# One scan for both directions of the S5 heads, and one modulation buffer lent by S5

## The chip, the cores and the metric

The kernel runs on one core of a Trainium2 chip. The metric is device time in microseconds (us) of one execution. TensorE (PE in the profile) multiplies matrices, VectorE (DVE) and ScalarE (ACT) work on tiles in on-chip memory, GpSimd (POOL) here clears memory and issues transfers, and SyncE (SP) issues transfers.

## What is computed

One layer of a hybrid backbone over 256 latent tokens and 256 context tokens of width 2048. Modulation vectors (shift, scale, gate) come from a matrix-vector product of SiLU(c) with a 2048 x 12288 matrix. A combined input projection feeds three mixers: S5 (a diagonal state space model), a convolution module, and a bidirectional mLSTM with four heads. An output projection, a SwiGLU block of width 5632 and a final norm follow.

The change is in S5 and in the buffers of the modulation. S5 has 32 groups of 16 channels with 64 complex states each, and it runs in both directions:

```
lam_bar = exp(lam * exp(log_step));  b_bar = ((lam_bar - 1) / lam)[..., None] * b
for di, reverse in enumerate((False, True)):
    h_c, h_fin = scan(einsum(uc, b_bar), lam_bar, 0, reverse)        # context
    h_x, _     = scan(einsum(ux, b_bar), lam_bar, h_fin, reverse)    # latent
    y_x += real(einsum(h_x, c_mat))
```

## The kernel before

**Weights.** A stream of 386 chunks of 8 weight tiles (512 KB each) is read by SP into `raw` (3 buffers). ScalarE rounds a chunk into `whi` (`split`, L263), VectorE makes the rest `wlo` = raw - whi, and TensorE multiplies with both. The buffers of `whi` and `wlo` are 3 deep, so ScalarE and VectorE run at most three chunks ahead of TensorE. The stream goes through the stages in a fixed order (`tile_order`): input projection for S5 and part of k, conv, rest of k, v, q, o, then the S5 gate, the output projection and the SwiGLU blocks.

**Order.** Work beside the stream is written as generators (`conv_job`, `s5_job`, `mod_job`, `gates_job`, `attention`). At each chunk `Sched.pump` runs steps of them by priority, as long as its own running sums of VectorE's and ScalarE's estimated work are less than 3,500 ns ahead of TensorE's. The helpers (`tt`, `stt`, `scan`, `act`) add the estimates. Afterwards the framework orders each engine's instructions once more by a simulated time, so the order on an engine is fixed when the program is built. Within an engine the instructions run in that order.

**S5.** `s5_params` makes the constants. `s5_moves` spreads the projection over `U` with eight copies on ScalarE and eight on VectorE. `s5_job` then goes through 16 pairs; a pair has two units `u`, one for each direction. `prep(p)` makes the input matrices (`bb`, then products with the powers `LW` into `Wb`), the output matrices (`cc`, products with `LC` into `Mb`) and a table of sines and cosines (`tab`). `main5(p)` multiplies on TensorE, rotates the result by the table on VectorE (`Vr`), runs the decay recurrence with `scan` (L191; four scans of 128 elements, one for each direction and for real and imaginary part), rotates back (`H1`, `H2`), and multiplies with `Mb` on TensorE. `prep(p + 1)` and `main5(p)` are stepped in turn. At the end of the job 16 copies on ScalarE and 16 on VectorE gather the result into `gT`.

**Modulation.** The first third of the matrix is read during the input projection in 64 pieces of 512 KB, into seven buffers: four of the tag `wm` and three slices of tiles that have no other use yet (`wm_extra`). The rest is read in 128 pieces during the later stages, through the four `wm` buffers alone, by POOL's queue (L337). `mod_job` goes through it in four quarters. Quarter 0 is multiplied on TensorE. In the quarters 1 to 3 ScalarE starts an accumulator `macc` and VectorE adds piece after piece to it (L179, two instructions to a piece); every eight pieces four transposes on TensorE close a block (L755). Each step takes two pieces and then issues the next two transfers. A transfer waits on POOL until its buffer has been read.

Of the kernel before, what the change touches and what calls it, by code (L numbers as in the profile page):

```python
# [10 lines left out]
F32 = mybir.dt.float32  # L11
# [139 lines left out]
def hybrid_layer_kernel(ctx: ExitStack, tc: tile.TileContext, xt, ctxt, wm1, wmr, wst, wg, bvrow, pvd, cstd, s5p, out):  # L151
# [169 lines left out]


    wm = {}
    NWM = 4

    wm_extra = [pre.tile([128, 2048], F32, name="wmu", tag="U"), pre.tile([128, 2048], F32, name="wmt", tag="T1")]
    wm_t1 = wm_extra[1]
    wm_extra = [wm_extra[0][:, 0:1024], wm_extra[0][:, 1024:2048], wm_extra[1][:, 1024:2048]]
    NWX = NWM + len(wm_extra)

    def wm_dma(key, src, q=None):
# [109 lines left out]

    LW = pre.tile([128, 2, 32, 4], F32, name="LW")
    LC = pre.tile([128, 2, 32, 5], F32, name="LC")
    s5c = pre.tile([128, 4, 32], F32, name="s5c")
    fre, fim, rho, frac = (s5c[:, i, :] for i in range(4))

    def s5_params():
        a = wm_t1[:, 0:1024].rearrange("p (a b) -> p a b", a=32)
# [70 lines left out]
        for o, s1, x1, x2, op in ((fre, 0, ar, ai, OP.add), (fim, 0, ai, ar, OP.subtract)):  # L519
            tt(o, x1, lre, OP.mult)  # L520
            tt(q, x2, lim, OP.mult)
            tt(o, o, q, op)
            tt(o, o, iv, OP.mult)
        yield

        L = [None] * 5
# [243 lines left out]
        while mst["q"] <= q:  # L770
            sc.step(mj)

    for _ in range(4):
        mod_dma()
    mj = sc.add(mod_job(), P_MOD)

# [10 lines left out]
                    acopy(o, i)  # L787

    def s5_job():
        Wb = pre.tile([128, 2, 2, 4, 32], F32, name="Wb", tag="s5W")  # L790
        Mbs = [pre.tile([128, 2, 2, 5, 32], F32, name="Mb", tag="s5M", bufs=2) for _ in range(2)]
        G.memset(Wb, 0.0)
        for m in Mbs:
            G.memset(m, 0.0)
        P5 = {}
# [1 line left out]
        def prep(p):  # L797
            u0 = 2 * p
            Mb = Mbs[p % 2]
            bc = pre.tile([128, 2, 4, 16], F32, name="bc", tag="s5bc")  # L800
            nc.gpsimd.dma_start(bc, s5p[p])
            yield S5_Y[0]
            bb = pre.tile([128, 2, 2, 2, 16], F32, name="bb", tag="s5bb")
            cc = pre.tile([128, 2, 2, 2, 16], F32, name="cc", tag="s5cc")

            def fb(f):
                return f[:, u0:u0 + 2][:, :, None, None].to_broadcast([128, 2, 2, 16])
            t1 = tmp(64).rearrange("p (u r c) -> p u r c", u=2, r=2)
            t2 = tmp(64).rearrange("p (u r c) -> p u r c", u=2, r=2)
            tt(t1, fb(fre), bc[:, :, 0:2, :], OP.mult)  # L810
            tt(t2, fb(fim), bc[:, :, 0:2, :], OP.mult)
            tt(bb[:, 0, :, 0, :], t1[:, :, 0, :], t2[:, :, 1, :], OP.subtract)
            tt(bb[:, 0, :, 1, :], t1[:, :, 1, :], t2[:, :, 0, :], OP.add)
            act(bb[:, 1, :, 0, :], bb[:, 0, :, 1, :], AF.Copy, scale=-1.0)
            acopy(bb[:, 1, :, 1, :], bb[:, 0, :, 0, :])
            acopy(cc[:, 0, :, 0, :], bc[:, :, 2, :])
            act(cc[:, 0, :, 1, :], bc[:, :, 3, :], AF.Copy, scale=-1.0)
            act(cc[:, 1], bc[:, :, 3:1:-1, :], AF.Copy, scale=-1.0)
            yield
            for L, n, x, dst in ((LW, 4, bb, Wb), (LC, 5, cc, Mb)):  # L820
                d1, d2 = (tmp(64 * n).rearrange("p (u s c) -> p u s c", u=4, s=n) for _ in range(2))
                for o, i in ((d1, 0), (d2, 1)):
                    for u in range(2):
                        tt(o[:, 2 * u:2 * u + 2], L[:, i, u0 + u, :][:, None, :, None].to_broadcast([128, 2, n, 16]),
                           x[:, i, u][:, :, None, :].to_broadcast([128, 2, n, 16]), OP.mult)
                tt(d1, d1, d2, OP.add)
                for hh in range(2):
                    acopy(dst[64 * hh:64 * hh + 64, :, :, :, 16 * hh:16 * hh + 16].rearrange("p u r s c -> p (u r s) c"),
                          d1[64 * hh:64 * hh + 64].rearrange("p u s c -> p (u s) c"))
                yield  # L830
            tab = pre.tile([128, 2, 2, 128], F32, name="tab", tag="s5tab")
# [25 lines left out]
            acopy(M2, ps[:, 0:128])  # L857
            P5[p] = (Mb, Wi, M2, tab)
            yield S5_Y[2]

        def main5(p):
            u0 = 2 * p
            Mb, Wi, M2, tab = P5.pop(p)
            ps = bbank()
            pv4 = ps.rearrange("p (u r k) -> p u r k", u=2, r=2)
            for d in range(2):
                r = U[:, p, :]
                if d:
                    r = r.rearrange("p (h k) -> p h k", h=2)[:, :, ::-1]
                for ri in range(2):  # L870
                    mm(pv4[:, d, ri, :], Wi[:, d, ri, :], r, True, True, native=True)
            Vr = pre.tile([128, 2, 2, 128], F32, name="Vr", tag="s5V")
            P2 = tmp().rearrange("p (u r k) -> p u r k", u=2, r=2)
            tt(Vr, pv4, tab[:, :, 0:1, :].to_broadcast([128, 2, 2, 128]), OP.mult)
            tt(P2, pv4[:, :, ::-1, :], tab[:, :, 1:2, :].to_broadcast([128, 2, 2, 128]), OP.mult)
# [8 lines left out]
            H1 = tmp(256).rearrange("p (u r k) -> p u r k", u=2, r=2)  # L884
            H2 = tmp(256).rearrange("p (u r k) -> p u r k", u=2, r=2)
            tt(H1, Vr[:, :, :, 63:127], tab[:, :, 0:1, 63:127].to_broadcast([128, 2, 2, 64]), OP.mult)
            tt(H2, Vr[:, :, ::-1, 63:127], tab[:, :, 1:2, 63:127].to_broadcast([128, 2, 2, 64]), OP.mult)
            tt(H1[:, :, 0, :], H1[:, :, 0, :], H2[:, :, 0, :], OP.subtract)
            tt(H1[:, :, 1, :], H1[:, :, 1, :], H2[:, :, 1, :], OP.add)
            yield S5_Y[3]  # L890
            ps = bbank()
            for d in range(2):
                for ri in range(2):
                    h = H1[:, d, ri, :]
# [531 lines left out]
```

## Time and profile before

| | |
|---|---|
| median of 3 runs | 1460.43 us (1458.61 to 1460.6) |
| profiled execution, its own time | 1461.92 us |
| span of its trace | 1460.2 us |
| TensorE busy | 1416.0 us (97%) |
| VectorE busy | 1058.8 us (73%) |
| ScalarE busy | 740.4 us (51%) |
| mean granted TensorE clock | 0.99 |

The span runs from the first to the last instruction; the profiled execution's own time is 1.72 us longer. Busy is the time in which an engine ran at least one instruction. Matmuls overlap, so a busy TensorE is not always TensorE at its peak. The shares are means over stages that differ.

### The profile page before, as it was taken

The page shows a single profiled execution, that of the slowest core. Times are in us where ns is not written, and L with a number is a line of the kernel's source. Part 1 is how long each engine was busy: PE and PEld are TensorE (multiplying, and loading weights), DVE is VectorE, ACT ScalarE, POOL GpSimd, SP SyncE. Part 2 cuts the span into 40 slices and gives each one's busy share as a digit, 9 for nine tenths or more (in the row PEclk, how much of TensorE's full clock was granted, in tenths as well). Part 3 has the DMA queues.
Part 4 walks back from the last instruction along what each step waited for, and adds up shares of the span by engine and source line. Part 5 has one row for each costly group of instructions (what it writes and reads, how often), then busy time and mean ns, then how long its engine had stood idle before and what let it go on. Part 6 is the DMA issues. An engine that isn't in the chain of part 4 may idle for free.

```text
span 1460.2 us, 25526 instructions
## 1 busy us (share of the span) xinstructions
PE 1416.0 (97%) x9856; PEld 1242.3 (85%) x9856; DVE 1058.8 (73%) x2104; ACT 740.4 (51%) x1279; POOL 107.3 (7%) x207
## 2 busy tenths in 40 slices
PE   6999899999999999999999999999999999999996
PEld 3888787887878999898998888888888888888885
DVE  7655699998988887888877778566555665556665
ACT  4334786654656555645555545433444334444353
POOL 1221111110001010011000010000000000000000
PEclk9999999999999999999999999999999999999998
DMA  9998464443436666689478787555555555555553
GB/s 365 359 359 300 156 234 142 164 165 117 143 120 226 219 238 236 243 310 343 145 234 278 277 299 240 187 189 186 189 188 187 187 188 188 188 188 188 188 177 112
DMA packets 87929, 315.31 MB, mean 216 GB/s; under 512 B 10096, under 2 KB 10880, under 8 KB 87808
## 3 DMA queue, kind: packets, MB, share of 16 engines
q1 hardware_dynamic: 60912, 216.67, 43.4%
q0 software_dynamic: 26896, 97.02, 18.8%
q8 instruction: 77, 1.26, 0.3%
q14 instruction: 44, 0.36, 0.1%
HBM read 311.55 MB, written 2.10 MB: 215 GB/s over the span
## 4 chain that ended last, share of the span: by engine, by line
PE 87%; DVE 5%; ACT 3%; DMA 2%; issue 1%; SPq 0%; DVEq 0%; ACTq 0%
PE ps_m L208 55%; PE ps_qk L208 20%; PE ps_b L208 12%; DMA raw<-in_wst_dram 1%; DVE tmp L168 1%; ACT whi L201 1%; DVE macc L179 1%; DVE wlo L168 1%; DMA tmp<-in_wg_dram 1%; ACT tmp L195 1%; PE ps_b L845 0%; ACT U L201 0%; PE ps_b L755 0%; DVE tmp L191 0%; DVE tmp L179 0%
## 5 line engine op out<-in xcount | busy, mean ns | idle before, releaser
L168 DVE TENSOR_TENSOR wlo<-raw,whi 128x1024 fp32r<-128x1024 f32 x386 | 471.3, 1222 | 268.0 <-ACT whi L201 264.4
L201 ACT CAST whi<-raw 128x1024 fp32r<-128x1024 f32 x386 | 403.8, 1047 | 478.8 <-PE ps_m L208 240.6
L208 PE MATMUL ps_m<-h,whi 128*128 128x512 f32 (+1 forms) x800 | 251.9, 369 | 3.5 <-ACT h L195 3.5
L208 PE MATMUL ps_m<-ffa,whi 128*128 128x512 f32 x704 | 248.8, 395 | 0.0
L208 PE MATMUL ps_qk<-h,whi 128*128 128x512 f32 (+1 forms) x688 | 233.2, 383 | 0.0
L208 PE MATMUL ps_m<-h,wlo 128*128 128x256 f32 x704 | 199.6, 284 | 0.0
L208 PE MATMUL ps_m<-ffa,wlo 128*128 128x256 f32 x704 | 198.9, 283 | 0.0
L208 PE MATMUL ps_m<-hx,whi 128*128 128x256 f32 x960 | 187.2, 291 | 5.5 <-ACT hx L195 3.6
L208 PE MATMUL ps_qk<-h,wlo 128*128 128x256 f32 x656 | 185.5, 283 | 0.0
L208 PEld LDWEIGHTS ps_m<-h,whi 128*128 128x128 f32 x800 | 144.9, 190 | 30.2 <-ACT h L195 4.0
L208 PEld LDWEIGHTS ps_m<-hx,whi 128*128 128x128 f32 x960 | 149.1, 190 | 24.7 <-issue 16.3
L208 PEld LDWEIGHTS ps_m<-ffa,whi 128*128 128x128 f32 x704 | 132.2, 188 | 32.2 <-issue 1.2
L208 PEld LDWEIGHTS ps_qk<-h,whi 128*128 128x128 f32 x688 | 127.2, 188 | 27.1
L179 DVE SCALAR_TENSOR_TENSOR macc<-wm,cs,macc 128x512 f32<-128x512 f32 x180 | 134.1, 745 | 6.2 <-ACT macc L195 3.8
L208 PE MATMUL ps_m<-hx,wlo 128*128 128x256 f32 x480 | 136.0, 284 | 0.0
L208 PEld LDWEIGHTS ps_m<-h,wlo 128*128 128x128 f32 x704 | 133.1, 189 | 0.0
L208 PEld LDWEIGHTS ps_m<-ffa,wlo 128*128 128x128 f32 x704 | 132.3, 188 | 0.1
L208 PEld LDWEIGHTS ps_qk<-h,wlo 128*128 128x128 f32 x656 | 123.3, 188 | 0.0
L337 POOL DMA_DIRECT2D wm<-in_wmr_dram x128 | 67.5, 528 | 607.7 <-DVE macc L179 431.3
L179 DVE SCALAR_TENSOR_TENSOR xres<-ps_m,mods,xres 128x256 f32<-128x256 f32 x160 | 76.9, 481 | 36.4 <-PE ps_m L208 34.4
L208 PEld LDWEIGHTS ps_m<-hx,wlo 128*128 128x128 f32 x480 | 91.2, 190 | 0.7 <-DVE wlo L168 0.7
L168 DVE TENSOR_TENSOR tmp<-tmp 128x256 f32<-128x256 f32 (+3 forms) x128 | 51.2, 410 | 6.1 <-ACT tmp L195 5.0
(268 smaller groups left out, 2135.7 us busy)
## 6 DMA issues: line engine op xcount, KB each, us to landing
raw<-in_wst_dram SPq DMA_DIRECT2D x386, 512.0 KB, 3.8
wm<-in_wmr_dram POOLq DMA_DIRECT2D x128, 512.0 KB, 5.3
wm<-in_wm_dram POOLq DMA_DIRECT2D x32, 512.0 KB, 7.0
wmu<-in_wm_dram POOLq DMA_DIRECT2D x16, 512.0 KB, 7.0
wmt<-in_wm_dram POOLq DMA_DIRECT2D x7, 512.0 KB, 5.8
wm<-in_wm_dram SPq DMA_DIRECT2D x5, 512.0 KB, 10.3
xr<-in_xt_dram SPq DMA_DIRECT2D x4, 512.0 KB, 6.0
cr<-in_ctxt_dram SPq DMA_DIRECT2D x4, 512.0 KB, 9.0
```

The lines of the kernel that those rows point to most:

```text
L168: V.tensor_tensor(out=o, in0=a, in1=b, op=op)
L179: V.scalar_tensor_tensor(o, a, s, b, op0=op0, op1=op1)
L195: i = S.activation(o, a, f, bias=bias, scale=scale)
L201: S.copy(o, a)
L208: i = P.matmul(o, lhsT=l, rhs=r, start=start, stop=stop, skip_group_check=sgc, **kw)
L337: i = (q or nc.gpsimd).dma_start(wm[key], src)
```

## The change

In `prep`, the product with `fre`, `fim` is written with a sign table (`nfim` = -`fim`), so that one addition replaces a subtraction and an addition; the products with `LW` and `LC` take both directions in one instruction (two of 256 or 320 elements instead of four of 128 or 160). The table `tab` gets a third part, the negated sine; its rounding step moves from ScalarE to the VectorE instruction that follows. In `main5`, the rotated values are laid out by real and imaginary part first, the two half additions of each rotation become one, and the four scans become one of 512 elements. Its decay comes from a table `rhot`, written for each pair by two ScalarE instructions; the table is zero at the first element of each of the four parts, where the recurrence starts anew. `Wb` and `rhot` share one tile `WR` of 1024 elements on the tag `s5W`. Before S5 starts, that memory serves as the seventh modulation buffer, and the tag `wm` has three buffers instead of four, also in the later quarters.

```diff
-    NWM = 4
+    NWM = 3
+    wm_s5 = pre.tile([128, 1024], F32, name="wms", tag="s5W")
-    wm_extra = [wm_extra[0][:, 0:1024], wm_extra[0][:, 1024:2048], wm_extra[1][:, 1024:2048]]
+    wm_extra = [wm_extra[0][:, 0:1024], wm_extra[0][:, 1024:2048], wm_extra[1][:, 1024:2048], wm_s5]
...
+        ts(nfim, fim, -1.0, OP.mult)
...
-    for _ in range(4):
+    for _ in range(NWM):
         mod_dma()
...
-        Wb = pre.tile([128, 2, 2, 4, 32], F32, name="Wb", tag="s5W")
+        WR = pre.tile([128, 1024], F32, name="WR", tag="s5W")
+        Wb = WR[:, 0:512].rearrange("p (u r s c) -> p u r s c", u=2, r=2, s=4)
+        rhot = WR[:, 512:1024].rearrange("p (r u k) -> p r u k", r=2, u=2)
-        G.memset(Wb, 0.0)
+        G.memset(WR, 0.0)
...
-            tt(t2, fb(fim), bc[:, :, 0:2, :], OP.mult)
-            tt(bb[:, 0, :, 0, :], t1[:, :, 0, :], t2[:, :, 1, :], OP.subtract)
-            tt(bb[:, 0, :, 1, :], t1[:, :, 1, :], t2[:, :, 0, :], OP.add)
+            tt(t2, s5c[:, 1:3, u0:u0 + 2].rearrange("p r u -> p u r")[:, :, :, None].to_broadcast([128, 2, 2, 16]),
+               bc[:, :, 1::-1, :], OP.mult)
+            tt(bb[:, 0], t1, t2, OP.add)
...
-                    for u in range(2):
-                        tt(o[:, 2 * u:2 * u + 2], L[:, i, u0 + u, :][:, None, :, None].to_broadcast([128, 2, n, 16]),
-                           x[:, i, u][:, :, None, :].to_broadcast([128, 2, n, 16]), OP.mult)
+                    tt(o, L[:, i, u0:u0 + 2, :][:, :, :, None].to_broadcast([128, 2, n, 32]),
+                       x[:, i].rearrange("p u r c -> p u (r c)")[:, :, None, :].to_broadcast([128, 2, n, 32]), OP.mult)
...
-            act(n, n, AF.Identity, bias=nmagic)
-            tt(t, t, n, OP.subtract)
-            act(tab[:, :, 1, :], t, AF.Sin, scale=2 * math.pi * (1 - 1e-7))
+            stt(t, n, MAGIC, t, OP.subtract, OP.subtract)
             act(n, t, AF.Abs)
-            act(tab[:, :, 0, :], n, AF.Sin, scale=-2 * math.pi, bias=halfpi)
+            act(tab[:, 2], t, AF.Sin, scale=2 * math.pi * (1 - 1e-7))
+            act(tab[:, 1], t, AF.Sin, scale=-2 * math.pi * (1 - 1e-7))
+            act(tab[:, 0], n, AF.Sin, scale=-2 * math.pi, bias=halfpi)
...
+            for d in range(2):
+                act(rhot[:, :, d, 1:128], one1[:, :, None].to_broadcast([128, 2, 127]), AF.Copy,
+                    scale=rho[:, u0 + d:u0 + d + 1])
...
-            tt(Vr[:, :, 0, :], Vr[:, :, 0, :], P2[:, :, 0, :], OP.add)
-            tt(Vr[:, :, 1, :], Vr[:, :, 1, :], P2[:, :, 1, :], OP.subtract)
+            tt(Vr, Vr, P2, OP.add)
             yield
-            for d in range(2):
-                for ri in range(2):
-                    scan(Vr[:, d, ri, :], rho[:, u0 + d:u0 + d + 1].to_broadcast([128, 128]), Vr[:, d, ri, :],
-                         0.0, OP.mult, OP.add)
+            Vf = Vr.rearrange("p r n -> p (r n)")
+            scan(Vf, WR[:, 512:1024], Vf, 0.0, OP.mult, OP.add)
...
-            tt(H1[:, :, 0, :], H1[:, :, 0, :], H2[:, :, 0, :], OP.subtract)
-            tt(H1[:, :, 1, :], H1[:, :, 1, :], H2[:, :, 1, :], OP.add)
+            tt(H1, H1, H2, OP.add)
```

## Rows read from the trace of the kernel before

**Rows 1.** Page, part 1: busy time, share of the span, instructions.

```profile
PE 1416.0 (97%) x9856; PEld 1242.3 (85%) x9856; DVE 1058.8 (73%) x2104; ACT 740.4 (51%) x1279; POOL 107.3 (7%) x207
```

**Rows 2.** Windows by stage: length, busy time (instructions) by engine, clock, DMA share, GB/s.

```profile
172.00:320.00 148.00, 145.44 (x1426) 125.07 (x1425) 142.88 (x403) 97.39 (x216) 20.15 (x39) 1.00 0.52 180
320.00:440.00 120.00, 119.49 (x783) 96.11 (x782) 103.92 (x261) 66.57 (x151) 9.46 (x18) 1.00 0.38 129
440.00:462.00 22.00, 20.29 (x139) 18.66 (x138) 19.47 (x36) 13.29 (x25) 2.12 (x4) 0.92 0.68 238
607.00:688.00 81.00, 80.92 (x684) 78.87 (x683) 72.45 (x101) 38.41 (x62) 12.67 (x24) 1.00 0.93 331
```

**Rows 3.** Timeline of TensorE: start, us; in brackets idle time before, releaser.

```profile
157.92 0.79 PE L208 MATMUL ps_b<-hx,whi 128*128 128x256 f32 x2 [4.07 <-ACT whi L201]
...
243.41 0.31 PE L998 MATMUL ps_b<-cst,rows 64*128 64x64 f32 x2 [1.44 <-DVE rows L168]
...
450.31 0.51 PE L208 MATMUL ps_m<-hx,whi 128*128 128x256 f32 x2 [1.71 <-ACT whi L201]
```

**Rows 4.** Windows: the ten us around the gap at 450 us.

```profile
450.00:460.00 10.00, 9.69 (x62) 8.82 (x63) 8.51 (x10) 2.70 (x5) 1.59 (x3) 0.83 0.75 261
```

**Rows 5.** Groups by form, VectorE, 172 to 440 us: count | busy us, mean ns | idle before.

```profile
L191 DVE TENSOR_TENSOR_SCAN Vr<-s5c,Vr 128x128 f32<-128x128 f32 x64 | 23.3, 405 | 0.0
L168 DVE TENSOR_TENSOR tmp<-LC,cc 128x160 f32<-128x160 f32 x60 | 16.4, 314 | 0.0
L168 DVE TENSOR_TENSOR tmp<-LW,bb 128x128 f32<-128x128 f32 x60 | 13.4, 276 | 0.0
L168 DVE TENSOR_TENSOR tmp<-tmp 128x256 f32<-128x256 f32 x30 | 12.5, 418 | 4.3 <-ACT tmp L195 4.3
L168 DVE TENSOR_TENSOR tmp<-tmp 128x128 f32<-128x128 f32 x32 | 7.7, 280 | 0.0
L168 DVE TENSOR_TENSOR tmp<-tmp 128x320 f32<-128x320 f32 x15 | 7.2, 479 | 0.0
L168 DVE TENSOR_TENSOR tmp<-s5c,bc 128x64 f32<-128x64 f32 x30 | 6.0, 215 | 0.0
L168 DVE TENSOR_TENSOR bb<-tmp 128x32 f32<-128x32 f32 x30 | 4.0, 172 | 0.0
...
L191 DVE TENSOR_TENSOR_SCAN tmp<-kc,tmp 32x256 f32<-32x256 f32 x4 | 2.7, 678 | 0.0
...
L168 DVE TENSOR_TENSOR rows<-rows,tmp 64x512 f32<-64x512 f32 x1 | 0.7, 676 | 0.0
```

**Rows 6.** Timeline of VectorE: three scans in a row, first start to last end.

```profile
191.01 1.05 DVE L191 TENSOR_TENSOR_SCAN Vr<-s5c,Vr 128x128 f32<-128x128 f32 x3
```

**Rows 7.** Groups by form, ScalarE, 172 to 440 us.

```profile
L195 ACT ACTIVATE tmp<-tmp,kc 128x256 f32<-128x256 f32 x30 | 15.3, 509 | 3.9 <-PE ps_b L208 1.9 <-DVE tmp L191 1.4
...
L195 ACT ACTIVATE tab<-tmp 128x256 f32<-128x256 f32 x15 | 6.2, 414 | 0.2
```

**Rows 8.** Timeline of ScalarE at the end of S5.

```profile
439.37 6.88 ACT L201 COPY gT<-U 32x128 f32<-32x128 f32 x16
446.27 1.05 ACT L201 CAST whi<-raw 128x1024 fp32r<-128x1024 f32 x1
```

**Rows 9.** Tile `Wb`, POOL's memset: ns min/median/max, first and last start.

```profile
L792 POOL MEMSET Wb<- x1: 524/524/524, 0.7 to 0.7; 128x512 f32 x1
```

**Rows 10.** Timeline of TensorE: two steps of modulation quarter 0.

```profile
203.96 1.06 PE L208 MATMUL ps_b<-wm,cs 128*32 128x512 f32 x8
...
210.84 1.07 PE L208 MATMUL ps_b<-wm,cs 128*32 128x512 f32 x8
```

**Rows 11.** Timeline of POOL: two transfers of the modulation issued in a row.

```profile
652.48 0.53 POOL L337 DMA_DIRECT2D wm<-in_wmr_dram  x1 [2.32 <-DVE macc L179]
655.34 0.53 POOL L337 DMA_DIRECT2D wm<-in_wmr_dram  x1 [2.33 <-DVE macc L179]
```

**Rows 12.** Timeline of VectorE: the two instructions that read one modulation piece.

```profile
576.43 1.53 DVE L179 SCALAR_TENSOR_TENSOR macc<-wm,cs,macc 128x512 f32<-128x512 f32 x2
```

**Rows 13.** Transfers of the modulation, 145 to 930 us: issue to landing.

```profile
DMA to landing us min/median/max: 3.6/5.3/8.9
```

More of the change, by code (lines that the diff above doesn't have):

```diff
@@ L443, in hybrid_layer_kernel @@
     LC = pre.tile([128, 2, 32, 5], F32, name="LC")
-    s5c = pre.tile([128, 4, 32], F32, name="s5c")
-    fre, fim, rho, frac = (s5c[:, i, :] for i in range(4))
+    s5c = pre.tile([128, 5, 32], F32, name="s5c")
+    fre, nfim, fim, rho, frac = (s5c[:, i, :] for i in range(5))
     def s5_params():
@@ L820, in prep @@
             for L, n, x, dst in ((LW, 4, bb, Wb), (LC, 5, cc, Mb)):
-                d1, d2 = (tmp(64 * n).rearrange("p (u s c) -> p u s c", u=4, s=n) for _ in range(2))
+                d1, d2 = (tmp(64 * n).rearrange("p (u s c) -> p u s c", u=2, s=n) for _ in range(2))
                 for o, i in ((d1, 0), (d2, 1)):
-                    for u in range(2):
-                        tt(o[:, 2 * u:2 * u + 2], L[:, i, u0 + u, :][:, None, :, None].to_broadcast([128, 2, n, 16]),
-                           x[:, i, u][:, :, None, :].to_broadcast([128, 2, n, 16]), OP.mult)
+                    tt(o, L[:, i, u0:u0 + 2, :][:, :, :, None].to_broadcast([128, 2, n, 32]),
+                       x[:, i].rearrange("p u r c -> p u (r c)")[:, :, None, :].to_broadcast([128, 2, n, 32]), OP.mult)
                 tt(d1, d1, d2, OP.add)
+                dr = d1.rearrange("p u s (r c) -> p u r s c", r=2)
                 for hh in range(2):
-                    acopy(dst[64 * hh:64 * hh + 64, :, :, :, 16 * hh:16 * hh + 16].rearrange("p u r s c -> p (u r s) c"),
-                          d1[64 * hh:64 * hh + 64].rearrange("p u s c -> p (u s) c"))
+                    acopy(dst[64 * hh:64 * hh + 64, :, :, :, 16 * hh:16 * hh + 16], dr[64 * hh:64 * hh + 64])
                 yield
-            tab = pre.tile([128, 2, 2, 128], F32, name="tab", tag="s5tab")
+            tab = pre.tile([128, 3, 2, 128], F32, name="tab", tag="s5tab")
             t, n = tmp(256).rearrange("p (u k) -> p u k", u=2), tmp(256).rearrange("p (u k) -> p u k", u=2)
@@ L864, in main5 @@
             ps = bbank()
-            pv4 = ps.rearrange("p (u r k) -> p u r k", u=2, r=2)
+            pv4 = ps.rearrange("p (r u k) -> p r u k", u=2, r=2)
             for d in range(2):
@@ L870, in main5 @@
                 for ri in range(2):
[L871 to L875, printed above, removed]
-            tt(Vr[:, :, 0, :], Vr[:, :, 0, :], P2[:, :, 0, :], OP.add)
@@ L877, in main5 @@
-            tt(Vr[:, :, 1, :], Vr[:, :, 1, :], P2[:, :, 1, :], OP.subtract)
+                    mm(pv4[:, ri, d, :], Wi[:, d, ri, :], r, True, True, native=True)
+            for d in range(2):
+                act(rhot[:, :, d, 1:128], one1[:, :, None].to_broadcast([128, 2, 127]), AF.Copy,
+                    scale=rho[:, u0 + d:u0 + d + 1])
+            Vr = pre.tile([128, 2, 256], F32, name="Vr", tag="s5V")
+            P2 = tmp().rearrange("p (r n) -> p r n", r=2)
+            pv3 = ps.rearrange("p (r n) -> p r n", r=2)
@@ L878, in main5 @@
+            tb = tab.rearrange("p a u k -> p a (u k)")
+            tt(Vr, pv3, tb[:, 0:1, :].to_broadcast([128, 2, 256]), OP.mult)
+            tt(P2, pv3[:, ::-1, :], tb[:, 1:3, :], OP.mult)
+            tt(Vr, Vr, P2, OP.add)
             yield
-            for d in range(2):
-                for ri in range(2):
-                    scan(Vr[:, d, ri, :], rho[:, u0 + d:u0 + d + 1].to_broadcast([128, 128]), Vr[:, d, ri, :],
-                         0.0, OP.mult, OP.add)
+            Vf = Vr.rearrange("p r n -> p (r n)")
@@ L883, in main5 @@
+            scan(Vf, WR[:, 512:1024], Vf, 0.0, OP.mult, OP.add)
             yield
[L884 to L887, printed above, removed]
-            tt(H1[:, :, 0, :], H1[:, :, 0, :], H2[:, :, 0, :], OP.subtract)
@@ L889, in main5 @@
-            tt(H1[:, :, 1, :], H1[:, :, 1, :], H2[:, :, 1, :], OP.add)
+            Vr = Vr.rearrange("p r (u k) -> p r u k", u=2)
+            H1 = tmp(256).rearrange("p (r u k) -> p r u k", u=2, r=2)
+            H2 = tmp(256).rearrange("p (r u k) -> p r u k", u=2, r=2)
+            tt(H1, Vr[:, :, :, 63:127], tab[:, 0:1, :, 63:127].to_broadcast([128, 2, 2, 64]), OP.mult)
+            tt(H2, Vr[:, ::-1, :, 63:127], tab[:, 2:0:-1, :, 63:127], OP.mult)
+            tt(H1, H1, H2, OP.add)
             yield S5_Y[3]
@@ L893, in main5 @@
                 for ri in range(2):
-                    h = H1[:, d, ri, :]
+                    h = H1[:, ri, d, :]
                     mm(ps[:, 0:64], Mb[:, d, ri, (1 - d):(5 - d), :].rearrange("p s c -> p (s c)"),
```

## The prediction, made before the change was run

> **What bounds the kernel now.** I read the page's busy times first: TensorE is busy 97% of the span [rows 1], and the chain that ended last lies almost wholly on it. So the number of its matmuls sets the time, and the change alters neither their number nor their shapes. What a change elsewhere can win or lose is the 44 us (1460.2 - 1416.0) in which TensorE is idle, and the clock that such idle time costs.
>
> Next I read the windows by stage, for the stages in which S5 runs. From 172 to 320 us VectorE is busy 142.88 of 148 us, from 320 to 440 us 103.92 of 120 [rows 2]. It is saturated there, yet TensorE is busy 145.44 of 148 and 119.49 of 120: the three chunks of lookahead cover it. The reader should see that a faster VectorE in this stretch buys nothing by itself, since TensorE hardly waits.
>
> Then I went through TensorE's timeline for the gaps. Most of the idle time is at the start and the end of the program, which S5 does not touch. Three gaps lie where S5 is at work [rows 3]: 4.07 us at 157.9, just after the input projection, behind the eight copies of `s5_moves` on ScalarE; 1.44 us at 243.4, where the gate rows come late from the saturated VectorE; and 1.71 us at 450.3, at the turn from v to q. Behind the last one the granted clock falls to 0.83 over ten us [rows 4], a mix of its levels 2.4 and 1.2 GHz, so the gap costs a further 10 x 0.17 = 1.7 us. That gap is S5's own doing: ScalarE spends 6.88 us in one go on the 16 `gT` copies at the end of the S5 job, and the next `whi` can start only behind them [rows 8].
>
> **The change, part by part.**
>
> *VectorE, for each of 16 pairs, by mean durations [rows 5].* `bb`: two of 215 and two of 172 ns become three of 215, -129. The `LW` products: four of 276 become two of 256 elements, taken at the 418 of that size, -268. The `LC` products: four of 314 become two of 320 elements at 479, -298. First rotation: two additions of 256 (418) become one of 512, whose nearest row on on-chip memory is 676, -160. The scans: the trace has none of 512. One of 128 takes 405, one of 256 takes 678, so 2.13 ns an element and 1,224 for 512; four at 405 are 1,620, -396. Its bounds are 1,620 (cost in proportion to length, no gain) and 676 (a plain addition of 512, -944); I take the slope, since it comes from two rows of the same operation. Second rotation: two of 280 become one of 418, -142. The rounding step stays one instruction of 256. Sum: -1,393 ns a pair, 22.3 us in all.
>
> This is too much, because neighbouring instructions overlap: three scans of 405 end 1.05 us after the first began [rows 6], so 0.08 us of each lies under the next. Ten instructions fewer on each of 16 pairs lose 160 x 0.0825 = 13.2 us of overlap, and 9.1 us remain. I take 9 us of freed VectorE time, with 22 as the upper bound. The Trainium skill says in Perfetto Trace Analysis, section Optimizing Scalar/DVE Operations, that an instruction on on-chip memory costs VectorE about 60 ns of engine time, and that its profiled latency is about twice that overhead; 160 x 60 ns would be an estimate of 9.6 us against 22.3 by durations. The overlap in the row sides with the smaller figure.
>
> *Where that time goes.* Freed VectorE time is not time of the kernel: TensorE covers it. What it moves is when S5 ends. S5's instructions share a VectorE that is busy 247 us between 172 and 440 us [rows 2], so 9 us less work lets the job end about 9 us earlier, near 430 instead of 439 us, inside the v stage. There a chunk lasts TensorE longer than in q (783 matmuls, mostly of 512 columns, in 120 us), and three chunks of lookahead cover a 6.88 us block on ScalarE. Gain: the 1.71 us gap and its 1.7 us of clock, 3.4 us. Below, the bound is nothing: the `gT` copies may fall on another turn. At the gates, VectorE is a few per cent less loaded; I take half of 1.44 us, 0.7, between 0 and 1.4.
>
> *ScalarE.* Two new instructions a pair for `rhot`, 254 elements each with a scale from memory. Nearest rows: 509 with an operand from memory, 414 without [rows 7]; I take 509. 32 x 0.51 = 16.3 us; one Identity (509) goes and one sine (414) comes, -1.5 us. Net about 15 us, on an engine busy 97.39 of 148 and 66.57 of 120 us [rows 2]: hidden in ScalarE's own idle time. But the one scan now waits for ScalarE, where the four read a constant. Queued behind a waiting scan on VectorE are the next `wlo`, for which TensorE waits. The rotation in front of the scan (three instructions, about 2 us) is its cover. I take 0; without cover, one `rhot` pair late by its own 1.0 us at every pair would take 16 us of VectorE's time.
>
> *POOL and start.* The memset takes 0.52 us for 512 elements [rows 9]; for 1,024 I take 1.05. It ran at 0.7 us; now it must wait until the last matvec has read the shared memory, before the first `Wb` copy. POOL's transfers queued behind it shift by 1 us at most, and POOL is idle most of the time. Cost 0, up to 1 us. `nfim` is one instruction of 32 elements, under 0.2 us, in the start stage. The first 64 pieces still have seven buffers: 0.
>
> *Three modulation buffers instead of four.* In quarter 0 TensorE itself reads the pieces. A step takes two; with three buffers one piece of the next step is issued only when this step has been read. The two closest steps start 6.9 us apart [rows 10], and a transfer lands after 5.3 us in the median, 8.9 at most [rows 13]; a wait comes only with a landing over some 6 us. In the quarters 1 to 3 VectorE reads a burst of eight pieces, one each 2.86 us [rows 11], 1.53 us to a piece [rows 12]. With four buffers a piece has 4 x 2.86 - 1.53 - 0.53 = 9.4 us to land, with three 6.5. The median fits, the slowest would make VectorE wait 2.4 us. The lookahead absorbs about 3 us (two chunks of about 2.86, less 1.05 for `whi` [rows 8] and somewhat more for `wlo`), but from 607 to 688 us VectorE is busy 72.45 of 81 us [rows 2], so it catches up slowly. I take +0.7 us, between 0 and 5 (two such waits in a burst, 4.8).
>
> *Sum* against the profiled execution: 1461.92 - 3.4 - 0.7 + 0.7 = 1458.5 us. That execution is 1.49 us above the median of the runs, so I forecast 1457.0 us for the median.
>
> **The rivals.**
>
> *Nothing on the path.* S5's position in the program is set by the order's estimates and by dependences, not by VectorE's real load; the job ends where it did, or its copies block another turn. For it: TensorE is idle under 0.6 us between 320 and 440. Time 1460.4 us, give or take 2.
>
> *Three buffers make VectorE late.* This one ends on the other side. It decides from the point at which landings in a burst exceed 6.5 us several times in a row: `macc` waits, the `wlo` behind it waits, and TensorE stops once the lag exceeds the 3 us of lookahead. Two waits of 2.4 us in a burst, less 3, are 1.8 us, and about as much again in clock, as at 450 us; alone 1464.0 us. For it: the stretch from 607 to 688 moves 331 GB/s at a DMA share of 0.93 [rows 2]. Against it: a median of 5.3, and fewer transfers in flight at once. In Perfetto Trace Analysis, section Identifying the Most-Contended Engine, the Trainium skill says that a gap that keeps repeating on the engine to be saturated can mean too few buffers. No such gap is in this trace with four.
>
> *ScalarE makes the scan late.* `rhot` comes behind a `whi` that waits for TensorE, the scan waits, and the first turn or the gates lose 2 us more with their clock: 1462.5 us.
>
> **How the numbers follow.** Forecast (S5 ends inside v) 0.44; nothing on the path 0.30; three buffers 0.18; late scan 0.08. The forecast's own range is 1454 to 1459.5. The range reaches down to 1452, which the forecast gives with all of the gates' gap and a shorter first turn, and up to 1464, the price of the three buffers. About 0.2% (2.9 us) is what a measurement of this kernel can tell from no change. Nearly all of the forecast and a little of the second case lie below 1457.5, and the last two cases mostly above 1463.3 or near it: faster 0.42, same 0.35, slower 0.23.
>
> **What would show it.** Right: VectorE's scans are 16 of about 1.2 us; S5's last instructions stand near 430 us; the gap at the turn to q is gone and the clock there is 1.00; waits of `macc` for transfers stay under 2 us each. Wrong: the `gT` copies still end in front of a gap; `macc` or the quarter 0 matmuls wait for transfers, with TensorE idle between 565 and 690 us; scans wait for ScalarE; or a gap of several us at another turn, the one at 158 us above all, since the whole order is laid out anew.

## The result, and the profile after it

The changed kernel takes 1473.93 us (median of 4 runs, 1472.72 to 1474.35) against 1460.01 us before (4 runs): 1.0095 times, 95% interval 1.0078 to 1.0113, so 13.9 us slower. The forecast was 1457.0 us with a range to 1464, so the time lies outside it. The profiled execution of before stands 1.9 us above its median, that of the changed kernel 0.1; profiles of other runs stand between 1.8 us below and 2.7 us above theirs, so a difference of two profiles can be off by some 4 us.

TensorE is the bound as before, with as many matmuls, and VectorE has become lighter by 7.6 us. Page of the changed kernel, part 1:

```profile
PE 1418.7 (96%) x9856; PEld 1242.1 (84%) x9856; DVE 1051.2 (71%) x1945; ACT 749.3 (51%) x1311; POOL 108.2 (7%) x207
```

The windows that answer to [rows 2] and [rows 4]:

```profile
172.00:320.00 148.00, 144.43 (x1370) 121.36 (x1363) 137.25 (x305) 100.04 (x229) 19.01 (x36) 1.00 0.50 176
320.00:440.00 120.00, 118.39 (x797) 95.19 (x796) 97.90 (x209) 75.19 (x181) 8.02 (x15) 1.00 0.34 114
440.00:462.00 22.00, 15.59 (x77) 13.56 (x76) 16.88 (x24) 5.35 (x6) 3.71 (x7) 0.84 0.64 220
607.00:688.00 81.00, 79.37 (x671) 77.59 (x670) 72.53 (x109) 39.41 (x72) 10.60 (x20) 1.00 0.82 289
450.00:460.00 10.00, 4.54 (x21) 4.57 (x22) 9.34 (x13) 0.13 (x1) 1.59 (x3) 0.66 0.65 237
```

VectorE is busy 137.25 and 97.90 us instead of 142.88 and 103.92, so the work did leave. The largest loss is in the third row: in the 22 us around the turn from v to q TensorE was busy 20.29 us before and 15.59 now, with the clock at 0.84 instead of 0.92. In the other three long stretches TensorE is busy 1.0 to 1.6 us less each. TensorE's gaps, beside [rows 3]:

```profile
158.62 0.51 PE L208 MATMUL ps_b<-hx,whi 128*128 128x256 f32 x2 [4.01 <-ACT whi L201]
...
244.55 0.31 PE L1005 MATMUL ps_b<-cst,rows 64*128 64x64 f32 x2 [1.25 <-DVE rows L168]
...
455.46 0.77 PE L208 MATMUL ps_m<-hx,whi 128*128 128x256 f32 x2 [6.41 <-DVE vx L168]
```

The gap of 1.71 us at the turn has become 6.41, and its releaser is no longer ScalarE's `whi` but `vx`: the four evictions of v, which copy finished sums out of the accumulators that q needs. VectorE's timeline there:

```profile
438.95 1.29 DVE L168 TENSOR_TENSOR gs<-gT,gs 128x512 fp32r<-128x512 f32 x2 [3.42 <-ACT gs L201]
440.16 0.15 DVE L168 TENSOR_TENSOR mods<-mods,pv 128x4 f32<-128x4 f32 x1
...
443.62 3.11 DVE L179 SCALAR_TENSOR_TENSOR macc<-wm,cs,macc 128x512 f32<-128x512 f32 x4
450.59 1.54 DVE L179 SCALAR_TENSOR_TENSOR macc<-wm,cs,macc 128x512 f32<-128x512 f32 x2 [3.87 <-DMA wm<-in_wmr_dram]
...
453.18 1.53 DVE L179 SCALAR_TENSOR_TENSOR macc<-wm,cs,macc 128x512 f32<-128x512 f32 x2
454.63 0.68 DVE L168 TENSOR_TENSOR vx<-ps_m,bvb 128x512 f32<-128x512 f32 x1
...
457.75 0.68 DVE L168 TENSOR_TENSOR vx<-ps_qk,bvb 128x512 f32<-128x512 f32 x1
```

v's matmuls end at 449.0 us. The first `vx` runs at 454.63, behind modulation instructions of which one pair waits 3.87 us for its piece. ScalarE shows why the modulation is there at that time:

```profile
428.18 0.28 ACT L763 ACTIVATE macc<-ps_b 128x128 f32<-128x128 f32 x1 [2.54 <-PE ps_b L757]
...
430.82 0.26 ACT L763 ACTIVATE macc<-ps_b 128x128 f32<-128x128 f32 x1
...
431.07 6.82 ACT L201 COPY gT<-U 32x128 f32<-32x128 f32 x16
437.92 0.28 ACT L763 ACTIVATE macc<-ps_b 128x128 f32<-128x128 f32 x1
...
460.52 1.05 ACT L201 CAST whi<-raw 128x1024 fp32r<-128x1024 f32 x1 [10.39 <-PE ps_m L208]
```

S5 does end early, as forecast (its last `U` at 427.74 us, 437.96 before). Its 16 `gT` copies now fall between the second and the third of the four sums that close a modulation block. The block closes at 440.16, with the write of `mods` shown above, and VectorE reads the eight pieces of the next block from 441.82 us on, over the turn. In the kernel before the block closed ahead of the copies, and the reading began 12 us earlier:

```profile
429.17 0.15 DVE L168 TENSOR_TENSOR mods<-mods,pv 128x4 f32<-128x4 f32 x1
...
429.84 0.74 DVE L179 SCALAR_TENSOR_TENSOR macc<-wm,cs,macc 128x512 f32<-128x512 f32 x1
```

The chain of waits through the turn says the same: the transfer, `macc`, `vx`, q.

```profile
443.40 2.03 issue
...
445.44 6.31 DMA wm<-in_wmr_dram
...
452.05 1.22 DVE wlo L168
453.27 0.67 DVE macc L179
...
454.63 0.69 DVE vx L168
...
455.46 6.58 PE ps_m L208 x36
```

The turn is not all. To see where time goes in every run, I cut each trace at five events that all of them have: the first and the last of the eight `kT` evictions, the 2nd and the 16th eviction of q, and the norm's sum on TensorE ahead of h, the input of the SwiGLU block. Lengths in us; old and new sequence are explained with their runs:

| kernel | to first kT | k | v and turn | q | gate, o | rest |
|---|---|---|---|---|---|---|
| before | 146.1 | 183.7 | 130.1 | 125.9 | 106.7 | 767.7 |
| changed | 146.8 | 189.1 | 134.2 | 126.5 | 107.7 | 767.9 |
| three buffers | 145.4 | 183.8 | 131.3 | 125.4 | 107.8 | 766.8 |
| old sequence, changed S5, three buffers | 146.5 | 183.7 | 127.9 | 125.3 | 108.0 | 768.9 |
| new sequence, S5 of before, four buffers | 144.2 | 185.1 | 133.7 | 125.1 | 106.4 | 768.2 |
| new sequence, S5 of before, three buffers | 146.1 | 192.6 | 133.0 | 127.0 | 107.8 | 767.5 |
| changed, block held | 146.2 | 188.3 | 125.6 | 125.2 | 108.6 | 782.6 |
| before, turn cleared | 146.5 | 183.6 | 126.8 | 126.9 | 106.4 | 769.0 |

Of the 12.0 us between the two profiles 5.4 are lost in k, 4.1 in v and the turn, 1.0 between q and the norm's sum, 1.5 in the other three parts. The profile of the kernel with the new sequence and four buffers stands 1.8 us below its median and that of before 1.9 above, so its row holds only 2.5 of the 6.6 us that it loses by the medians.

### The profile page after: what moved, and what is told of

Same layout as the page of the kernel before. It is cut to its first block, busy times and chain, and to the rows that moved or that the text cites. A ratio compares the mean times of both kernels' runs of the same rounds, so it can differ in the third digit from the quotient of the medians.

```text
span 1472.2 us, 25391 instructions
## 1 busy us (share of the span) xinstructions
PE 1418.7 (96%) x9856; PEld 1242.1 (84%) x9856; DVE 1051.2 (71%) x1945; ACT 749.3 (51%) x1311; POOL 108.2 (7%) x207
## 4 chain that ended last, share of the span: by engine, by line
PE 77%; issue 8%; DVE 6%; DMA 4%; ACT 3%; POOL 1%; SPq 0%; DVEq 0%; POOLq 0%; ACTq 0%
PE ps_m L208 49%; PE ps_qk L208 19%; PE ps_b L208 9%; DMA wm<-in_wmr_dram 1%; DVE tmp L168 1%; DVE wlo L168 1%; DVE macc L179 1%; DMA raw<-in_wst_dram 1%; ACT whi L201 1%; DMA tmp<-in_wg_dram 1%; DMA wm<-in_wm_dram 1%; ACT tmp L195 1%; ACT U L201 0%; DVE tmp L191 0%; DMA xr<-in_xt_dram 0%
## 5 line engine op out<-in xcount | busy, mean ns | idle before, releaser
L179 DVE SCALAR_TENSOR_TENSOR XB<-XB,pv 128x256 f32<-128x256 f32 x120 | 54.3, 479 | 0.5
```

Of the source, the lines that this page charges most:

```text
L179: V.scalar_tensor_tensor(o, a, s, b, op0=op0, op1=op1)
```

## The experiments

Three theories. **T1**: three buffers instead of four cost the time, by waits for modulation pieces. **T2**: the sequence of S5's pairs, the modulation and `vx`, which the planner lays out anew, costs it. **T3**: the new S5 instructions cost it themselves, above all the two `rhot` writes. One row speaks for T3: in the changed kernel the `rhot` write of the next pair waits for the scan that still reads the table (groups of ScalarE, 172 to 440 us):

```profile
L195 ACT ACTIVATE WR<-kc,s5c 128x254 f32<-128x254 f32 x30 | 14.8, 503 | 24.5 <-DVE Vr L191 24.5
```

### The buffers alone

```diff
-    NWM = 4
+    NWM = 3      # and wm_s5, Wb as in the change; S5 as before
```

> The kernel before with one edit alone: three modulation buffers instead of four (S5's block lends the eighth early buffer), S5 as it was, so that VectorE's instructions keep their order. T1 (the buffers cost the time: macc waits for pieces at the turn of v to q): 1460 plus the 3.9 us that VectorE waited for a piece there, plus the clock that follows, 1464 to 1474. T2 (the shift of a modulation burst in front of the four vx evictions costs it): 1459 to 1462, since the order stays as before. T3 (the rhot writes on ScalarE cost it): 1459 to 1462, there is no rhot here.

Measured 1462.73 us (11 runs), ratio 1.0017, interval 1.0007 to 1.0028: some 2.5 us, a sixth of the loss. It lies between the ranges of the three theories, nearer to those of T2 and T3. VectorE's waits for pieces, 1.0 us in one wait before, in this kernel:

```profile
DVE macc L179 <- DMA wm<-in_wmr_dram: 9.5, 15, 1.6
```

So 8.5 us more of waiting become 2.5 us; the rest is covered. To see how steep this is, two buffers:

> The kernel before with two modulation buffers instead of four (the early extra pieces as with three), S5 and the sequence as before. A piece now has only the time of about one step to land. T1 in its form that the buffers cost by the waits of VectorE: with three VectorE waited 9.5 us for pieces against 1.0 and the kernel lost some 2.5; with two the waits grow several times, 1470 to 1500. If VectorE's waits are mostly hidden: 1463 to 1468.

Measured 1509.77 us, ratio 1.0345 (1.0324 to 1.0367), above both ranges.

```profile
DVE macc L179 <- DMA wm<-in_wmr_dram: 54.5, 42, 3.9
```

VectorE waits 53.5 us more and 49.8 us are lost. TensorE's own idle time grows by 33.7 us (span less busy: 77.9 against 44.2), and its mean clock falls from 0.990 to 0.982 in the two profiled runs. The short waits of three buffers are mostly hidden, those of two are not. The order isn't quite as before here: some 130 of VectorE's 2,104 instructions stand elsewhere.

### The `rhot` wait

```diff
-  rhot = WR[:, 512:1024] as (r, u, k)
+  rhots = [WR[:, 512:768], WR[:, 768:1024]]     # even and odd pairs
-  scan(Vf, WR[:, 512:1024], Vf, 0.0, OP.mult, OP.add)
+  for ri in range(2):
+      scan(Vr[:, ri, :], rhots[p % 2], Vr[:, ri, :], 0.0, OP.mult, OP.add)
```

> The changed kernel with two decay tables of 256 columns, used in turn by even and odd pairs, each read by two scans of 256 (re and im) instead of one of 512: the rhot write of the next pair no longer waits for the scan of this one; the scans get longer by 16 x some 0.06 us, about 1 us in all. T3: the 24.5 us that ScalarE stood before its rhot writes go, S5's pairs are no longer slowed, and the some 5 us that TensorE lost between 243 and 449 us come back: 1466 to 1470, and the modulation burst may come back to its place. T2: only as far as the burst at the turn of v to q moves by it: if vx still stands behind it 1473 to 1475, if not about 1467. T1: 1474, the buffers are still three.

Measured 1474.52 us, 1.0091 (1.0072 to 1.0110). The wait is gone, and the time is not:

```profile
L195 ACT ACTIVATE WR<-kc,s5c 128x127 f32<-128x127 f32 x28 | 10.0, 393 | 2.0 <-DVE Vr L191 1.8
```

T3's 1466 to 1470 is missed, so T3 in this form falls. The planner's sequence moved too (a twelfth S5 pair falls into k, where the other kernels of the table have eleven), so the run alone doesn't say more.

### The turn of the changed kernel

```diff
-        yield 1000        # after S5's Gelu, ahead of the gT copies
+        yield 12000
```

> The changed kernel with S5's last copies (gT) issued later by 12 us of planned TensorE time instead of 1, so that the modulation piece's sums stand ahead of them on VectorE and its burst starts earlier, as in the kernel before; S5 and the three buffers as changed. T2: the TensorE gap of 6.41 us at the turn of v to q falls to 2 or less and the clock behind it stays up: 1473.9 less 4.5 less 1.5, 1466 to 1469. T1: the burst still waits for its pieces, now in front of vx as well: 1472 to 1476. T3: no change in S5's pairs, 1472 to 1475.

Measured 1469.41 us, 1.0063 (1.0047 to 1.0080): 4.5 us less than the changed kernel, nearest to T2's range. But the gap at the turn is 3.81 us instead of 6.41, more than the 2 that T2 allowed. Now all four `vx` by force in front of the block:

```diff
+            while (q, b) == (1, 1) and not mst.get('vx'):
+                yield 500        # vx and this block's macc in program order
```

> The changed kernel with the order at the turn of v to q set by hand: the modulation block of that place is held until the four vx evictions are issued, and those and its macc steps keep that order; S5 and the three buffers as changed. T2: vx follows v's last matmuls at once, the gap of 6.41 us falls to under 1 and the clock behind it stays up: 1465 to 1468. T1: the pieces come no faster, but nothing of v waits for them now, so the waits land in q: 1468 to 1474. T3: 1472 to 1475.

Measured 1478.90 us, 1.0126 (1.0110 to 1.0142), slower still and above all three ranges. T2's number failed, its place did not: windows of the 40 us from 440, then TensorE's timeline ahead of h.

```profile
440.00:480.00 40.00, 40.00 (x274) 36.69 (x273) 28.08 (x48) 17.70 (x28) 3.17 (x6) 1.00 0.64 219
...
708.74 1.12 PE L763 MATMUL ps_b<-cst,macc 128*128 128x128 f32 x4 [14.13 <-DVE macc L181]
```

The turn costs nothing any more (33.59 us of 40 in the changed kernel, clock 0.91), and TensorE came to the norm's sum at 693.91 us instead of 704.26. But the held block closes at 497.8 us instead of 471.6, the modulation stays late, and h waits 14.13 us for it. Moving an instruction off a turn has a price where its result falls due. Faster steps behind the hold did not catch up:

> The changed kernel with the modulation block held behind the four vx evictions at the turn of v to q, and the modulation's steps after it planned 9.0 us of TensorE time apart instead of 10.0 until quarter 2 is done, so that the sums lost at the turn are caught up. T2 (the burst in front of vx is the main loss): the wait of 14.1 us for the late modulation before h goes, the gain at the turn stays; TensorE reached the norm's sum at 693.9 us there against 704.3 in the changed kernel, so 1473.9 less 10.4, 1463 to 1466. T1 (three buffers can't feed it): the denser steps wait for their pieces and the loss comes back elsewhere, 1468 to 1478.

Measured 1482.27 us (1.0156), above both ranges: TensorE waits 9.68 us ahead of h, and there are new waits in the gate stage. Holding only three of the four steps, packed behind `vx`:

> The changed kernel with only the last three of the four steps of the modulation block at the turn held behind the four vx evictions, and issued 2 us of planned TensorE time apart right behind them, so that the block isn't late for the blocks after it. T2: the gap of 6.41 us at the turn is under 1 and nothing is late before h: 1473.9 less 10.4, 1463 to 1466. T1: the packed steps wait for their pieces with three buffers and delay q's splits, 1467 to 1473. T3: 1470 to 1474.

Measured 1467.79 us, 1.0055 (1.0043 to 1.0067), 6.1 us less than the changed kernel. That is in T1's range and 1.8 us above T2's. The gap at the turn is gone, TensorE waits 1.69, 1.17 and 1.39 us for `macc` where three later blocks close, and k still takes 190.7 us.

### Halves of the change

> The changed kernel with the products of before (eight a pair, and the two subtractions and additions of bb): one scan of 512 with the decay table, sine table with both signs and three buffers stay. On VectorE the vx evictions stand between the macc steps as in the kernel before. T2: a gap of 1.7 to 3.5 us at the turn, 1461 to 1466. T3: the rhot writes still wait for the scans, kT's last tile comes 5 us late as in the changed kernel, 1466 to 1470. T1: 1462 to 1465, the price of the buffers alone.

Measured 1467.30 us, 1.0053 (1.0039 to 1.0067): a turn with 3.59 us of gap, and k 190.7 us long. That is in T3's range and 1.3 us above T2's. But here too a twelfth S5 pair falls into k, so its length can't be compared with the others, and the run doesn't decide.

> The kernel before with only the power products of both directions in one instruction each (four instead of eight a pair), four scans, four buffers, no decay table. All theories: VectorE is some 8 us lighter in S5. If a lighter VectorE were worth time by itself: 1455 to 1458. T2: only what stands in front of vx at the turn counts; here the four evictions stand together behind S5's last split, which waits for ScalarE: 1459 to 1464. T1 and T3: 1457 to 1460, neither buffers nor rhot are touched.

Measured 1463.15 us, 1.0028 (1.0019 to 1.0037): slower, with four fewer VectorE instructions a pair as the only edit; T2's range alone holds it. It is hard to see how the instructions themselves could cost that, and it led to the next runs.

### Sequence and instructions apart

The helpers add each instruction's estimated cost to the planner's sums. The change books 620 ns less VectorE and 806 ns more ScalarE a pair. The sums alone can be changed, with no instruction touched. In what follows, old and new sequence mean the order that comes out when S5 is booked at the costs of before or of the change:

```diff
 # changed kernel, old plan                     # kernel before, new plan
+  sc.dve += 62    # bb, rotations 1 and 2      +  sc.dve -= 62
+  sc.dve += 124   # LW, LC                     +  sc.dve -= 124
+  sc.dve += 186   # scan                       +  sc.dve -= 186
+  sc.act -= 806   # rhot                       +  sc.act += 806
```

> All instructions and buffers of the changed kernel, but S5's pairs are booked in the planner at the costs of before (620 ns of VectorE more and 806 ns of ScalarE less a pair), so that the pairs, the modulation steps and vx are issued in the sequence of before. T2 (the sequence costs the time, not the instructions): the loss of the k stage and of the turn of v to q goes, the price of three buffers stays, 1459 to 1464. T3 (the new instructions' own waits cost it, the rhot writes above all): the k stage is as slow as in the changed kernel, 1466 to 1474. T1: 1462 to 1466.

> All instructions and the four buffers of the kernel before, but S5's pairs are booked in the planner at the costs of the change (620 ns of VectorE less and 806 ns of ScalarE more a pair), so that the pairs, the modulation steps and vx are issued in the sequence of the changed kernel. T2: the sequence alone brings the loss, 1464 to 1472; its k stage ends later and the gap at the turn grows. T1 and T3: neither the buffers nor the instructions change, 1459 to 1461.

> All instructions of the kernel before, three modulation buffers, and S5 booked in the planner at the costs of the change, so that it issues in the changed kernel's sequence: nothing of the new S5 is in it. If sequence and buffers only add: 1459.7 plus 6.6 plus 2.5 to 3.1, 1468 to 1470. If they make the whole loss together, without the new instructions: 1472 to 1475. If the new instructions are needed for the rest: 1466 to 1470.

Measured, against the kernel before:

| | S5 of before | changed S5 |
|---|---|---|
| old sequence, four buffers | 1 | does not fit |
| old sequence, three buffers | 1.0017 (1.0007 to 1.0028) | 1.0026 (1.0017 to 1.0034) |
| new sequence, four buffers | 1.0052 (1.0040 to 1.0064) | does not fit |
| new sequence, three buffers | 1.0098 (1.0083 to 1.0114) | 1.0095 (1.0078 to 1.0113) |

The second and the last row decide between T2 and T3. The left kernel of the last row (1475.75 us) has not one instruction of the new S5; its page shows VectorE's count and busy time of before:

```profile
PE 1422.2 (96%) x9856; PEld 1242.0 (84%) x9856; DVE 1058.9 (72%) x2104; ACT 741.0 (50%) x1279; POOL 107.7 (7%) x207
```

It loses as much as the change. And the changed S5 with the old sequence loses no more than the buffers alone by what can be measured (the intervals overlap), although its `rhot` writes wait longer than in the changed kernel:

```profile
L195 ACT ACTIVATE WR<-kc,s5c 128x254 f32<-128x254 f32 x30 | 14.8, 504 | 29.5 <-DVE Vr L191 29.5
```

So T2 holds, with T1 as a part: the sequence alone takes 0.52%, the buffers alone 0.17%, both together 0.98%, 4 us more than their sum (some 1 to 7 us, an estimate from the three intervals). Of the three cases that I had put down for both together the second comes nearest; that they only add was wrong.

How good these comparisons are can be seen in the traces, instruction by instruction. With three buffers alone, all 2,104 VectorE and all 1,279 ScalarE instructions stand in the order of the kernel before. The new booking alone moves some 370 of VectorE's and some 185 of ScalarE's, and with three buffers it gives the same order as with four, but for two VectorE instructions. So down the left column of the table only the buffers differ within one order: one buffer less costs 0.17% in the old order and 0.46% in the new one (1.0098 against 1.0052). Across the columns the orders are alike and not the same: the bookings are equal, and the framework's second ordering still has other instructions to order. The left kernel of the last row ends S5 later than the changed kernel (its `gT` copies begin at 440.61 us, there at 431.07), its gap at the turn is the smaller one, and it loses 8.9 us in k where the changed kernel loses 5.4:

```profile
455.55 0.48 PE L208 MATMUL ps_m<-hx,whi 128*128 128x256 f32 x2 [2.55 <-DVE vx L168]
```

What is shown, then, is that booking and buffers are enough for a loss of this size, and that within either booking the new instructions add nothing that can be measured. The changed kernel loses its time partly in other places, so how its own 13.9 us divide between order and buffers is not shown.

The extra of sequence and buffers together is seen in k (185.1 us with four buffers, 192.6 with three), where TensorE works on quarter 0: its matmuls take longer in all, and wait for pieces. TensorE's groups from 243.4 to 336 us, before, with the new sequence and four buffers, and then with both:

```profile
L208 PE MATMUL ps_b<-wm,cs 128*32 128x512 f32 x64 | 9.6, 605 | 0.0
```

```profile
L208 PE MATMUL ps_b<-wm,cs 128*32 128x512 f32 x64 | 10.6, 604 | 1.2 <-issue 1.0 <-DMA wm<-in_wmr_dram 0.2
```

```profile
L208 PE MATMUL ps_b<-wm,cs 128*32 128x512 f32 x64 | 12.5, 633 | 3.7 <-DMA wm<-in_wmr_dram 2.6 <-issue 1.1
```

Against before, the last has 2.9 us more of work and 3.7 of waits, of the 8.9 us that k lost there. In the changed kernel these 64 matmuls take 12.3 us, 2.7 of the 5.4 us that k lost, and waits for S5's `tmp` and for `kT` are about 1 us longer. The other 1.7 us in k stay open.

### What the lighter VectorE and the turn are worth

The merged products (the second of the halves above), booked at the old cost, four buffers:

> The kernel before with the power products of both directions in one instruction each (248 ns of VectorE less a pair as the planner books it), booked at the old cost, so that the sequence and the four buffers stay as before: the lighter VectorE alone. If VectorE's work in S5 is on the path: 1455 to 1458. If it is off the path: 1459 to 1461, as the kernel before.

Measured 1460.43 us, 1.0003 (0.9994 to 1.0012): nothing, with 3.5 us less of VectorE's busy time (1055.3 us against 1058.8). Then the turn of the kernel before, first with the block held and with part of it held:

> The kernel before with the same edit at the turn alone (block held behind vx, steps after it 9.0 us apart), four buffers and S5 as it was. T2: its own gap of 1.71 us at the turn and the 1.7 us of clock behind it go: 1460.0 less 3.4, 1456 to 1458. If the held block makes the modulation late before h: 1460 or more.

> The kernel before with the same edit at the turn (three of the block's four steps held behind vx, packed behind it), four buffers. T2: the 1.71 us of gap at its turn and the 1.7 us of clock behind it go, 1455.5 to 1458. If the packed steps delay q's weight splits instead: 1460 to 1464.

Measured 1473.77 us (1.0100; 8.37 us of waiting ahead of h for the late modulation) and 1460.79 us (1.0014, 1.0006 to 1.0023; with `vx` early, the gap is 3.20 us behind the `gT` copies on ScalarE). With those copies behind q's first splits as well:

```diff
-                        acopy(o, i)             # gT
+                        acopy(o, i, pin=True)   # job resumed 30 us later
```

> The kernel before with the turn of v to q cleared on both engines: three of the modulation block's four steps behind the four vx evictions, and S5's gT copies on ScalarE issued 30 us of planned TensorE time later, behind the first weight splits of q. If the gap of 1.71 us and the 1.7 us of clock behind it were the turn's price: 1460 less 3.4, 1455.5 to 1458. If the work only moves into q and costs there: 1459 to 1463.

Measured 1459.79 us, 0.9996 (0.9988 to 1.0005). The 40 us from 440, before and in this kernel:

```profile
440.00:480.00 40.00, 38.29 (x264) 35.26 (x263) 33.50 (x70) 24.49 (x52) 4.23 (x8) 0.96 0.69 231
```

```profile
440.00:480.00 40.00, 37.73 (x280) 35.48 (x279) 38.87 (x67) 25.40 (x49) 6.36 (x12) 1.00 0.81 287
```

The clock is 1.00 instead of 0.96 and "v and turn" is 3.3 us shorter, near the 3.4 us forecast for it. But q is 1.0 us longer (waits of 0.98 and 1.19 us of TensorE for `macc` and for VectorE's attention work), and the rest 1.3 us. Whether these 1.3 belong to it or to the execution I can't tell. The runs show no gain.

> The kernel before with the turn of v to q cleared as in the experiment on the turn and the merged power products booked at the old cost. By the experiments so far neither was worth anything that could be measured: 1459 to 1461. If a lighter VectorE pays once the turn is clear: 1455 to 1458.

Measured 1459.41 us, 0.9994 (0.9983 to 1.0004). None of the versions that were run beats the kernel before by what can be measured.

## Why the prediction was wrong

- **A faster VectorE buys nothing by itself here**: right, and shown for four of the ten instructions a pair (1.0003 booked at the old cost, four buffers). For all ten together it was seen with three buffers alone: 1.0026 with the old sequence, where the buffers by themselves have 1.0017.
- **VectorE's sum**: right, 1.5 us too high. The groups of the changed kernel that answer to [rows 5]:

```profile
L191 DVE TENSOR_TENSOR_SCAN Vr<-WR,Vr 128x512 f32<-128x512 f32 x16 | 19.5, 1218 | 0.0
L168 DVE TENSOR_TENSOR tmp<-LC,cc 128x320 f32<-128x320 f32 x30 | 14.3, 483 | 0.0
...
L168 DVE TENSOR_TENSOR tmp<-LW,bb 128x256 f32<-128x256 f32 x30 | 11.9, 420 | 0.0
...
L168 DVE TENSOR_TENSOR Vr<-Vr,tmp 128x512 f32<-128x512 f32 x16 | 10.9, 684 | 0.0
```

  The scan of 512 was taken at 1,224 ns and takes 1,218; the others are within 8 ns. VectorE's busy time fell by 7.6 us where 9.1 were forecast; the 22.3 us by durations were far off. The estimate of 9.6 us from the Trainium skill (Perfetto Trace Analysis, Optimizing Scalar/DVE Operations) was near too.
- **S5 ends near 430 us**: the number is right (427.74), but that VectorE's lighter load brought it is not shown. The `gT` copies begin at 431.07 us in the changed kernel and at 439.37 before. The changed S5 with the old sequence begins them at 433.04, and the S5 of before with the new sequence and four buffers, where VectorE is no lighter, at 432.83. Either can do it.
- **Gain of 3.4 us at the turn**: here the prediction failed. It took the end of S5 for the only thing that moves. The order is made from estimates of every instruction's cost, so the new costs re-place S5's pairs, the modulation steps and `vx` over some 300 us. The prediction knew this: "nothing on the path" says that the order's estimates set S5's place, and its last sentence warns that the whole order is laid out anew. It gave that no price: the sum has no term for it, and a rival "another piece of work lands on the turn" is missing. Measured, the new sequence costs 0.52% with four buffers (7.6 us by the ratio, 6.6 between the medians), and in the changed kernel the gap at the turn grew from 1.71 to 6.41 us, behind `vx`. Even with the changed S5 booked as before a gap of 1.85 us stays there, now behind `vx` too; only the clock keeps to 1.00, and v and turn is 2.2 us shorter. The size of the turn itself was right: 3.3 us where it was cleared. But it was no gain of the kernel, since none was left in the time (1459.79 us, 0.9996).
- **Three buffers at +0.7 us**: undersized. Alone they cost some 2.5 us, inside the bounds 0 to 5, and with the new sequence 0.46%, some 6.7 us, outside them. The rival "three buffers make VectorE late" gave 1464.0 us for them alone, and 1462.73 were measured. Its mechanism (`macc` waits for pieces) was there, 9.5 us of waits, but its point of decision was not what counted: with three buffers alone, three landings in a row took 7.2 to 7.9 us from 573.6 us on and four 6.6 to 7.8 from 614.8 on, and the late pieces were mostly covered. In the changed kernel one wait of 3.87 us stood ahead of `vx` and was not covered. The prediction had named `wlo` as what is queued behind it, not `vx`. The Trainium skill says in Perfetto Trace Analysis, Optimization Strategy (not in the section that the prediction named, which stands ahead of it), that a gap repeating on the engine to be saturated can mean too few buffers. Here the repeating gaps are on VectorE, which feeds that engine: 15 waits with three buffers, 42 with two. TensorE's idle time goes from 44.2 us to 45.6 and 77.9, so on the saturated engine the sign hardly shows with three.
- **ScalarE hidden, late scan at nothing**: right in size (`rhot` 503 ns, forecast 509; no scan waited for it). The wait that came is the opposite one, the write behind the scan, 24.5 us on ScalarE. It cost nothing that could be measured either (29.5 us of it with the old sequence, at 1.0026).
- **Gates**: 1.25 us instead of 1.44, so 0.2 where 0.7 was taken. **POOL**: the memset took 0.96 us, hidden.
- **Not tried**: the changed S5 with four buffers; it needs 3.1 KB a partition more than there is.

## What to carry to other kernels

Where a planner orders the work by booked costs, a lighter instruction is also an edit of the order: price that first, by booking the new cost on the old instructions, or the old cost on the new ones, and look at what lands in front of the evictions at each turn. One buffer less may look nearly free by its waits as long as the lookahead covers them, and cost more than twice as much once the order changes with it (0.17% and 0.46% here). A gap that is cleared is worth only what is not due elsewhere: the held block came back as 14 us ahead of h.

## What the runs showed that was not expected

The matmuls of 32 columns (128*32 in the rows), of which four stand side by side on TensorE, cost by the group and not by their number. TensorE's timeline of the changed kernel:

```profile
303.80 1.06 PE L208 MATMUL ps_b<-wm,cs 128*32 128x512 f32 x8
...
305.88 1.05 PE L208 MATMUL ps_b<-wm,cs 128*32 128x512 f32 x4
```

Eight in one group take 1.06 us, four 1.05, and two at 262.37 us 1.04. The ends are modelled, but the starts say the same: the next matmul starts 1.00 us after the first of the eight, and 0.98 us after that of the four and of the two. A modulation step that the order splits into two groups costs TensorE 1 us more, with no wait to be seen, because both groups count as busy. That is how k can lose 2.7 us while TensorE looks as busy as before.
